# A two-layer trunk: where the weights of the next layer are split and where its residual is made

## The chip, the cores and the metric

The kernel runs on one core of a Trainium2 chip. The metric is the time of one execution on the device in microseconds, smaller is better; the figure given is the median of several runs. TensorE is the matmul engine (PE in the rows), VectorE is DVE, ScalarE is ACT, GpSimd is POOL, and SyncE (SP) only issues transfers here.

## What is computed

The reference, cut to the latent stream. All arrays are float32.

```python
alpha = (2 * DEPTH) ** 0.25                         # DEPTH = 2
h_lat = x                                           # [1, 512, 1024]
for layer in range(DEPTH):
    m_lat = split(silu(c) @ w_mod[layer] + b_mod[layer], 6)
    u_lat = h_lat * (1 + m_lat[1]) + m_lat[0]
    if layer == 0:                                  # attention beside a pooling mixer
        y_lat = attn_pool_mixer(u_lat, u_ctx, ...) @ w_out
    else:                                           # short gated convolution
        b_gate, c_gate, x_in = split(u_lat @ w_conv_in, 3)
        z = conv3(c_gate * x_in)                    # depthwise, width 3
        y_lat = (b_gate * z) @ w_conv_out
    h_lat = layer_norm(alpha * h_lat + m_lat[2] * y_lat, ln_mix_g, ln_mix_b)
    f_lat = expert_choice_ffn(h_lat * (1 + m_lat[4]) + m_lat[3], ...)   # 16 experts, 64 tokens each
    h_lat = layer_norm(alpha * h_lat + m_lat[5] * f_lat, ln_ffn_g, ln_ffn_b)
return h_lat
```

The convolution layer takes the normalised output of layer 0 twice: through the modulation into its input product, and, times alpha, as the residual that is added to the output projection.

## The kernel before

The 512 tokens are four row tiles of 128 (index `t`), the 1024 channels eight blocks of 128 (index `k`). Large weights stream from HBM into blocks of 16 KB per partition. `self.queue` lists what is loaded, in order; `next_load(b)` takes the next entry and loads it into block `b` as soon as the last reader of `b` is done, or, where the entry is `None`, puts `b` on the list `freed`. All these loads go through SyncE's queue. The order of instructions on each engine is the program's order (the schedule is written by hand); engines wait for one another only through data and buffers.

A float32 product of full precision outside the experts is made of three fast matmuls (`mm3`): both operands are split into a high part (a cast on ScalarE) and a low part (a subtract on VectorE or GpSimd). `split` does this (L247 the cast, L248 the subtract), and the three matmuls are L252 to L254.

**End of layer 0.** `moe(0)` runs 16 experts. In the last one, while the hidden copy `hT` waits for the down product, `ln_row` (L283, L285) spreads the LN gain and bias over all partitions: four matmuls into one PSUM bank and one ScalarE copy, twice for each of the two rows. They land in a spare block. Then the down product is made in two column halves (L1431), its sums are added to `A` (L1454, on VectorE; L1442 on GpSimd for two tiles), and the final norm follows in two halves of two row tiles each. Each tile has a reciprocal root (two ScalarE activations, then a Newton step on VectorE, L268 to L273) and a norm, L1563: `H = (A - mean) * rstd`, without the gain and bias.

`open_conv`, called before those norms, makes the first of the convolution's split weights: `prep_conv(i)` splits weight block `i` ([128 x 1024], three blocks per entry `ci0`, `ci1`, ... of the queue) into a ring of four slots. Blocks 0, 1 and 2 are split there, their subtracts on GpSimd; block 3 comes after the first two norms, also on GpSimd. `post1(b, g)` then turns half `b` of the tokens around: four transposes on TensorE, two scaled activations on ScalarE (L1607) and a split (`u1`, the low part on VectorE), for four groups `g`. `self.residual(t, g1)` computes `A = H * gain + bias` (both times alpha) with four GpSimd operations per row tile (L293, L294), tiles 0 and 1 after the first `post1`s, 2 and 3 at the very end.

**Layer 1.** `layer1_mixer` loops over `f` (8) and `b` (3): `conv_in` makes the product for weight block `i = 3f + b`, then `prep_conv(i + 3)` refills the ring, one step of the modulation's list `steps` runs (sums of gate weights on VectorE, L355 and L357; every third step a matmul `mod_b` or `mod_pc`), and VectorE works the convolution's taps (L1681 to L1687). For `f = 0` the products of the first 256 tokens run ahead of the rest. `mix_out` is the output projection: `project(t, n0, n1)` is one row tile times one column half, `evac` adds the result to the residual (L1092, L1096) and takes statistics; eight passes in all. At its start `others()` splits eight more weight tiles.

Of the kernel before, what the change touches and what calls it, by code (L numbers as in the profile page):

```python
# [16 lines left out]
P = 128  # L17
# [173 lines left out]
class Trunk:  # L191
    def __init__(self, nc, tc, ins, out, ctx):
        self.nc, self.tc, self.ins, self.out, self.ctx = nc, tc, ins, out, ctx
        self.n = 0
        self.last_tile = {}

# [253 lines left out]
    def run(self):  # L450
# [29 lines left out]
        def experts(l):  # L480
            return [item(f"{n}{l}_{e}_{h}", ins["wdl"][l, h] if (e, n) == (NE - 1, "d") else ins["w" + n][l, e, h])
                    for e in range(NE) for n in ("g", "u", "d") for h in range(2)]
# [6 lines left out]
        self.queue = ([m[0][i] for i in TN['order']] + [None] * 2 + m[1][:4] + experts(0) + ci[:4] + [None] * 4  # L489
                      + m[1][4:6] + [ci[4]] + m[1][6:8] + [ci[5], m[1][8], ci[6]] + m[1][9:11] + [ci[7], m[1][11]] + wco  # L490
# [546 lines left out]
    def mix_out(self, layer, aH, aL, w, others, sp, wk, mods, free):  # L1037
# [122 lines left out]

        for t in range(TT):
            p_y = project(t, 0, 512)
            if t == 0:
                consts()
                p_ls = [self.bank(q, (P, P), "p_l") for q in "gu"]
                p_f = [None] * TT
                p_a = self.bank("d", (64, 2 * P), "p_a")
            else:
                trans(t - 1, 0, 4)
            if t > 1:  # L1170
                logits(t - 2, 0)
            evac(t, 0, 512, p_y)
            if t == 0:
                others()
            step(t)
        for b in free[0]:
            self.next_load(b)
        for t in range(TT):
            lt = t == TT - 1
            for n0, n1 in ((512, 768), (768, 1024)) if lt else ((512, 1024),):  # L1180
# [12 lines left out]
                evac(t, n0, n1, p_y)  # L1193
                if n0 == 512 and lt:
                    softmax(0)()
# [80 lines left out]
    def moe(self, layer):  # L1276
# [6 lines left out]
        with tc.tile_pool(name=f"ex{layer}", bufs=2) as wk:  # L1283
# [87 lines left out]
            for e in range(NE):  # L1371
# [33 lines left out]
                if self.spare and not gb:  # L1405
                    gb += [self.spare[:, v * D:v * D + D] for v in range(2)]
                    g1 = [side(v) for v in gb]
                    for v in range(2):
                        self.ln_row(4 * layer + 2 + v, g1[v], 1.0 if last else ALPHA)
# [149 lines left out]
            else:  # L1559
# [12 lines left out]
                self.rs.append(self.prep_conv(3, nc.gpsimd))  # L1572
# [8 lines left out]
                for t in range(2):  # L1581
                    self.residual(t, g1)
# [6 lines left out]
                self.conv_in(self.p_c[1], self.rs[1], 0, 256)  # L1589
                for g in range(4):  # L1590
                    self.post1(1, g, wk)
                for t in range(2, TT):
                    self.residual(t, g1)
# [23 lines left out]
    def open_conv(self):  # L1617
# [3 lines left out]
        self.rs = [self.prep_conv(i, self.nc.gpsimd) for i in range(3)]  # L1621
        self.next_load(self.w["ci0"][1])
# [9 lines left out]
    def layer1_mixer(self):  # L1632
        nc, tc, ins, base = self.nc, self.tc, self.ins, self.base
        uH, uL = self.u1
        with tc.tile_pool(name="l1", bufs=1) as pool:
# [4 lines left out]
            hx = base.tile([P, TT, D], F32, tag="H", name="H")  # L1640
            self.H = hx
# [19 lines left out]
            for f in range(KO):  # L1661
# [4 lines left out]
                for b in range(3):  # L1666
                    i = 3 * f + b
                    p_b = self.bank(name=f"p_c{b}") if f else p_c[b]
                    self.conv_in(p_b, rs[i], 0 if f else 256, 512)
                    if i and i + 3 < 3 * KO:  # L1670
# [57 lines left out]
```

## Time and profile before

| what | value |
| --- | --- |
| median of 3 runs | 1466.15 us (1464.01 to 1473.38) |
| the profiled execution's own time | 1466.89 us |
| its span (first to last instruction) | 1465.0 us |
| TensorE busy | 1371.5 us |
| VectorE busy | 709.1 us |
| ScalarE busy | 335.2 us |
| GpSimd busy | 270.9 us |
| mean granted TensorE clock | 0.97 |

The table by stretches gives for each engine the busy us in a stretch and in brackets how many instructions, then the granted TensorE clock as a share of full speed. In the timeline each line has its start, its duration (or the extent of several merged instructions, with their count), engine, line of the kernel, operation, result and operands, and, in square brackets, how long the engine was idle before it and what ended that.

### The profile page before, as it was taken

To read this page: it belongs to the slowest core of one execution; us is meant where nothing else is said; L and a number is where in the kernel's file an instruction comes from. 1 tells how busy PE (TensorE), PEld (TensorE's weight loads), DVE (VectorE), ACT (ScalarE), POOL (GpSimd) and SP (SyncE) were. 2 spreads that over 40 slices of the span, in tenths; PEclk is the share of its full clock that TensorE was granted. 3 is DMA by queue.
4 is the path that set the end of the run, shared out by engine and by line. 5 is a ranking of instruction groups with operands and counts; after the bars stand their busy time and mean duration, and the time that the engine had idled before them with its cause. 6 is when DMAs were issued, how large, how long until landed. Compare 5 with 4: busy or idle time off the path is not lost.

```text
span 1465.0 us, 17481 instructions
## 1 busy us (share of the span) xinstructions
PE 1371.5 (94%) x7180; PEld 765.1 (52%) x7180; DVE 709.1 (48%) x1158; ACT 335.2 (23%) x661; POOL 270.9 (18%) x242
## 2 busy tenths in 40 slices
PE   7989998899999999999959999999999999999993
PEld 4866547654444444543348787764454454444332
DVE  3684768813343333342476799661243243343246
ACT  3455661311111011111043222231111111111013
POOL 2321628450000000000065445005000000000003
PEclk9989999999999999999979999999999999999996
DMA  9437337889999999999962554749999999999991
GB/s 370 159 133 284 140 138 318 310 325 407 428 425 427 427 427 427 426 426 427 417 271 98 230 211 172 287 191 376 427 427 426 426 428 426 427 426 427 426 388 57
DMA packets 42527, 490.35 MB, mean 335 GB/s; under 512 B 4752, under 2 KB 5200, under 8 KB 13136
## 3 DMA queue, kind: packets, MB, share of 16 engines
q1 hardware_dynamic: 41856, 486.10, 80.6%
q10 hardware_dynamic: 592, 3.15, 0.6%
q8 instruction: 56, 0.92, 0.3%
q14 instruction: 23, 0.19, 0.0%
HBM read 487.13 MB, written 2.10 MB: 334 GB/s over the span
## 4 chain that ended last, share of the span: by engine, by line
PE 66%; DMA 16%; DVE 13%; ACT 2%; issue 2%; SPq 0%; DVEq 0%; ACTq 0%
PE p_g L1331 11%; PE p_d L1331 11%; PE p_u L1331 10%; DMA blk<-wu 5%; DMA blk<-wg 5%; DMA blk<-wd 5%; PE p_ga_g L1309 5%; PE p_sc_sc L1359 3%; PE p_c_sc L252 2%; PE p_c_sc L253 2%; PE p_c_sc L254 2%; PE p_y_sc L252 2%; PE p_y_sc L254 2%; PE p_y_sc L253 2%; PE p_o L945 1%
## 5 line engine op out<-in xcount | busy, mean ns | idle before, releaser
L1331 PE MATMUL p_u<-blk,xe 128*64 128x512 f32 x1024 | 226.3, 593 | 6.3 <-DMA blk<-wu 6.3
L1331 PE MATMUL p_g<-blk,xe 128*64 128x512 f32 x1024 | 226.3, 593 | 2.2 <-ACT xe L1318 2.2
L1331 PE MATMUL p_d<-blk,hT 128*64 128x512 f32 x960 | 215.2, 601 | 0.0
L1391 DVE TENSOR_TENSOR rows<-sg,p_u 128x512 f32<-128x512 f32 x32 | 22.0, 688 | 325.4 <-PE p_u L1331 315.3
L1362 DVE SCALAR_TENSOR_TENSOR A<-p_sc_sc,gates,A 128x512 f32<-128x512 f32 x240 | 163.2, 743 | 6.1 <-PE p_sc_sc L1359 6.1
L1331 PEld LDWEIGHTS p_u<-blk,xe 128*64 128x64 f32 x1024 | 72.4, 137 | 154.5 <-issue 140.0
L1331 PEld LDWEIGHTS p_g<-blk,xe 128*64 128x64 f32 x1024 | 72.6, 137 | 147.1 <-issue 140.0
L1421 POOL COPY m5c<-m5b 64x256 f32<-64x256 f32 x8 | 3.2, 394 | 718.0 <-PE p_ga_g L1309 717.6
L1331 PEld LDWEIGHTS p_d<-blk,hT 128*64 128x64 f32 x960 | 66.6, 138 | 131.4 <-issue 131.2
L1318 ACT ACTIVATE xe<-p_ga_g,FG 128x128 f32<-128x128 f32 x112 | 42.2, 457 | 306.8 <-PE p_ga_g L1309 306.8
L1309 PEld LDWEIGHTS p_ga_g<-sel,H 128*128 128x128 f32 x896 | 104.2, 192 | 3.0 <-issue 0.8
L1309 PE MATMUL p_ga_g<-sel,H 128*128 128x128 f32 x896 | 104.7, 275 | 0.0
L1353 ACT CAST yp<-rows 64x512 fp32r<-64x512 f32 (+1 forms) x68 | 40.2, 591 | 272.8 <-DVE rows L1350 272.0
L1350 DVE TENSOR_TENSOR rows<-p_d,m5b 128x512 f32<-128x512 f32 x30 | 20.8, 692 | 136.3 <-PE p_d L1331 136.3
L1359 PE MATMUL p_sc_sc<-yp,st 128*128 128x512 f32 x240 | 72.8, 421 | 1.0 <-DVE A L1362 1.0
L248 POOL TENSOR_TENSOR blk<-blk,blk 128x1024 fp32r<-128x1024 f32 (+1 forms) x25 | 59.7, 2405 | 67.8 <-ACT blk L247 67.8
L252 PE MATMUL p_c_sc<-blk,blk 128*128 128x512 f32 x168 | 67.7, 403 | 0.0
L253 PE MATMUL p_c_sc<-blk,blk 128*128 128x512 f32 x168 | 65.9, 392 | 0.0
L254 PE MATMUL p_c_sc<-blk,blk 128*128 128x512 f32 x168 | 65.8, 392 | 0.0
L1359 PEld LDWEIGHTS p_sc_sc<-yp,st 128*128 128x128 f32 x240 | 40.6, 188 | 34.3 <-issue 24.3
L1354 DVE TENSOR_TENSOR yp<-rows,yp 64x512 fp32r<-64x512 f32 (+1 forms) x68 | 45.6, 671 | 25.3 <-ACT yp L1353 24.2
L357 DVE SCALAR_TENSOR_TENSOR rows<-blk,cond,rows 128x512 f32<-128x512 f32 x49 | 56.2, 1147 | 1.5
(402 smaller groups left out, 1999.3 us busy)
## 6 DMA issues: line engine op xcount, KB each, us to landing
blk<-wg SPq DMA_DIRECT2D x60, 2048.0 KB, 28.0
blk<-wu SPq DMA_DIRECT2D x60, 2048.0 KB, 22.1
blk<-wd SPq DMA_DIRECT2D x56, 2048.0 KB, 26.3
blk<-wmod SPq DMA_DIRECT2D x23, 2048.0 KB, 8.7
blk<-wci SPq DMA_DIRECT2D x8, 1536.0 KB, 12.2
blk<-wd SPq DMA_DIRECT2D x8, 1024.0 KB, 7.2
blk<-wg SPq DMA_DIRECT2D x8, 1024.0 KB, 8.7
blk<-wu SPq DMA_DIRECT2D x16, 512.0 KB, 22.9
```

Of the source, the lines that this page charges most:

```text
L248: (eng or nc.vector).tensor_tensor(lo, src, hi.bitcast(F32), ALU.subtract)
L252: mm(out, ah, bh, start=start, stop=False)
L253: mm(out, ah, bl, start=False, stop=False)
L254: mm(out, al, bh, start=False, stop=stop)
L357: nc.vector.scalar_tensor_tensor(a, W[:, k], c, a, ALU.mult, ALU.add)
L1309: nc.tensor.matmul(pg[:, j - j0], H[:, t, j * P:(j + 1) * P], sels[g][:, t, e0:e1].rearrange("p e s -> p (e s)"), start=t == 0, stop=t == ...
L1318: nc.scalar.activation(o, pg[:, j - j0], AF.Identity, bias=self.FG[:, 1, j:j + 1], scale=self.FG[:, 0, j:j + 1])
L1331: nc.tensor.matmul(o[64 * hf:64 * hf + 64], lhs(k), W[:, kk, hf * 512:hf * 512 + 512], start=k == 0, stop=k == KO - 1)
L1353: nc.scalar.copy(yp[r, hf], ye[r])
L1354: nc.vector.tensor_tensor(yp[q, hf], ye[r], yp[r, hf].bitcast(F32), ALU.subtract)
L1359: nc.tensor.matmul(pp[hf], st[:, t * P:(t + 1) * P], yp[:, hf], start=True, stop=True)
L1362: nc.vector.scalar_tensor_tensor(a, pp[hf], self.gateT[:, t, e:e + 1], a, ALU.mult, ALU.add)
```

## The change

Four things change. In the queue the fourth convolution weight (`ci3`) and the first gate weight of layer 1 (`m[1][4]`) trade places. At the end of layer 0 only weight block 0 is split beside the norms; GpSimd takes block 1 after a one-element copy that reads the second norm's result, VectorE takes block 2 after the second pair of norms, and GpSimd block 3 between the second and third group of the second half. The load that reuses `ci0`'s block follows block 2. The residual leaves GpSimd: the old `H` is kept under the name `A`, the new scratch tile takes the buffer of the old `A`, and VectorE multiplies and adds in place, in eight pieces of one row tile and one column half, two before the first pass of `mix_out` and one after each evacuation. The LN rows for it are made in the convolution's steps 1 and 2 instead of in the last expert of layer 0.

```diff
--- before.py
+++ after.py
@@ -193,6 +193,7 @@
         self.nc, self.tc, self.ins, self.out, self.ctx = nc, tc, ins, out, ctx
         self.n = 0
         self.last_tile = {}
+        self.resid = []
 
 
     def cv(self, name, rows=P):
@@ -486,8 +487,8 @@
         wco = [item(f"wco{h}", ins["wco"][h]) for h in range(2)]
         self.item, self.mitems = item, m
         self.w, self.freed = {}, []
-        self.queue = ([m[0][i] for i in TN['order']] + [None] * 2 + m[1][:4] + experts(0) + ci[:4] + [None] * 4
-                      + m[1][4:6] + [ci[4]] + m[1][6:8] + [ci[5], m[1][8], ci[6]] + m[1][9:11] + [ci[7], m[1][11]] + wco
+        self.queue = ([m[0][i] for i in TN['order']] + [None] * 2 + m[1][:4] + experts(0) + ci[:3] + m[1][4:5] + [None] * 4
+                      + [ci[3], m[1][5], ci[4]] + m[1][6:8] + [ci[5], m[1][8], ci[6]] + m[1][9:11] + [ci[7], m[1][11]] + wco
                       + experts(1))
         self.layer0_mixer()
         self.moe(0)
@@ -1158,6 +1159,11 @@
             for i, s in plan[q] if mods else ():
                 mods[i][s]()
 
+        def resid(n=1):
+            for _ in range(min(n, len(self.resid))):
+                self.resid.pop(0)()
+
+        resid(2)
         for t in range(TT):
             p_y = project(t, 0, 512)
             if t == 0:
@@ -1170,6 +1176,7 @@
             if t > 1:
                 logits(t - 2, 0)
             evac(t, 0, 512, p_y)
+            resid()
             if t == 0:
                 others()
             step(t)
@@ -1191,6 +1198,7 @@
                 else:
                     softmax(1)()
                 evac(t, n0, n1, p_y)
+                resid()
                 if n0 == 512 and lt:
                     softmax(0)()
             if lt:
@@ -1402,11 +1410,11 @@
                 if e < NE - 1:
                     scatters(2)
                 st = scatter_sel(e)
-                if self.spare and not gb:
+                if last and self.spare and not gb:
                     gb += [self.spare[:, v * D:v * D + D] for v in range(2)]
                     g1 = [side(v) for v in gb]
                     for v in range(2):
-                        self.ln_row(4 * layer + 2 + v, g1[v], 1.0 if last else ALPHA)
+                        self.ln_row(4 * layer + 2 + v, g1[v], 1.0)
                 lhs = lambda k: hT[:, k % 4, (k // 4) * CAP:(k // 4) * CAP + CAP]
                 yp = wk.tile([P, 2, 512], F32R, name="yp", bufs=1)
                 if e < NE - 1:
@@ -1569,7 +1577,9 @@
                 for t in range(2):
                     newton[t]()
                     norm(t)
-                self.rs.append(self.prep_conv(3, nc.gpsimd))
+
+                nc.gpsimd.tensor_copy(self.smc[:, 3:4], H[:, 1, D - 1:D])
+                self.rs.append(self.prep_conv(1, nc.gpsimd))
                 for t in (2, 3):
                     nc.vector.bn_stats(bst[:, t, 0], A[:, t, 0:512])
                 total(2)
@@ -1578,8 +1588,6 @@
                 total(3)
                 for g in range(2, 4):
                     self.post1(0, g, wk)
-                for t in range(2):
-                    self.residual(t, g1)
                 rstd(2, 4)()
                 for t in (2, 3):
                     norm(t)
@@ -1587,10 +1595,12 @@
                 self.p_c = [self.bank(q, name="p_c") for q in "gud"]
                 self.conv_in(self.p_c[0], self.rs[0], 0, 256)
                 self.conv_in(self.p_c[1], self.rs[1], 0, 256)
+                self.rs.append(self.prep_conv(2))
+                self.next_load(self.w["ci0"][1])
                 for g in range(4):
                     self.post1(1, g, wk)
-                for t in range(2, TT):
-                    self.residual(t, g1)
+                    if g == 1:
+                        self.rs.append(self.prep_conv(3, nc.gpsimd))
 
     def post1(self, b, g, wk):
 
@@ -1618,8 +1628,7 @@
 
         self.rblk, self.ublk = self.freed[-4:-2], self.freed[-2:]
         self.ring = [self.block(b, F32R).rearrange("p (i s k c) -> p i s k c", i=2, s=2, k=KO) for b in self.rblk]
-        self.rs = [self.prep_conv(i, self.nc.gpsimd) for i in range(3)]
-        self.next_load(self.w["ci0"][1])
+        self.rs = [self.prep_conv(0, self.nc.gpsimd)]
         self.u1 = [self.block(b, F32R).rearrange("p (k n) -> p k n", k=KO) for b in self.ublk]
 
     def prep_conv(self, i, eng=None):
@@ -1637,8 +1646,17 @@
             gL = pool.tile([P, KO, S], F32R, name="gL")
             rx, ry = self.rblk
 
-            hx = base.tile([P, TT, D], F32, tag="H", name="H")
-            self.H = hx
+            hx = base.tile([P, TT, D], F32, tag="A", name="A")
+            self.H, self.A = hx, self.H
+            gb = [[pool.tile([P, 512], F32, name=f"l1gb{v}{h}") for h in range(2)] for v in range(2)]
+
+            def residual(h, t):
+                a = self.A[:, t, h * 512:h * 512 + 512]
+                nc.vector.tensor_tensor(a, a, gb[0][h], ALU.mult)
+                nc.vector.tensor_tensor(a, a, gb[1][h], ALU.add)
+
+            self.resid = [lambda q=q: residual(*divmod(q, TT)) for q in range(2 * TT)]
+
             self.load_gates(1, hx[:, 3])
             cbs, zbs = ([hx[:, a, i * 512:i * 512 + 512] for i in range(2)] for a in range(2))
             tb = hx[:, 2, 0:S + 2]
@@ -1667,6 +1685,8 @@
                     i = 3 * f + b
                     p_b = self.bank(name=f"p_c{b}") if f else p_c[b]
                     self.conv_in(p_b, rs[i], 0 if f else 256, 512)
+                    if i in (1, 2):
+                        self.ln_row(1 + i, gb[i - 1], ALPHA)
                     if i and i + 3 < 3 * KO:
                         rs.append(self.prep_conv(i + 3, nc.gpsimd if i > 1 else None))
                     elif i + 3 >= 3 * KO:
```

## Rows read from the trace of the kernel before

**Rows 1.** The page's list of engines: busy us (share of the span) and instructions.

```profile
PE 1371.5 (94%) x7180; PEld 765.1 (52%) x7180; DVE 709.1 (48%) x1158; ACT 335.2 (23%) x661; POOL 270.9 (18%) x242
```

**Rows 2.** Stretches: busy us of PE, PEld, DVE, ACT, POOL; PE clock; DMA share; GB/s.

```profile
746.00:755.50 9.50, 0.01 (x1) 0.00 (x0) 9.19 (x15) 3.33 (x7) 9.01 (x4) 0.53 0.72 266
...
765.80:767.80 2.00, 0.00 (x0) 0.00 (x0) 1.93 (x6) 0.79 (x3) 1.34 (x2) 0.81 0.00 0
767.80:774.70 6.90, 6.87 (x35) 6.88 (x36) 2.68 (x7) 0.00 (x0) 4.57 (x4) 0.56 0.01 2
...
818.50:902.00 83.50, 83.50 (x386) 69.54 (x385) 72.46 (x75) 17.49 (x21) 42.13 (x20) 1.00 0.56 221
...
921.00:972.00 51.00, 50.38 (x309) 41.10 (x309) 28.43 (x79) 12.53 (x32) 0.72 (x3) 1.00 0.52 193
...
957.00:961.00 4.00, 4.00 (x20) 3.30 (x19) 1.24 (x8) 1.65 (x3) 0.00 (x0) 1.00 0.00 0
```

**Rows 3.** Waits of TensorE, 740 to 830: total us, times, longest.

```profile
PE p_tr_sc L1603 <- DVE H L1563: 12.4, 2, 9.6
PE p_c_g L253 <- DVE blk L248: 3.5, 4, 2.1
PE mod_b_sc L415 <- DVE rows L357: 2.1, 1, 2.1
```

**Rows 4.** The timeline of VectorE (start, us, ...): norms and Newton steps of both halves.

```profile
749.35 1.09 DVE L268 SCALAR_TENSOR_TENSOR rs_t<-l_r 128x1 f32<-128x1 f32 x1
...
750.66 2.08 DVE L273 TENSOR_TENSOR l_r<-l_r,rs_t 128x1 f32<-128x1 f32 x1
752.77 2.79 DVE L1563 TENSOR_SCALAR H<-A,l_nm,l_r 128x1024 f32<-128x1024 f32 x1
...
756.96 1.84 DVE L1563 TENSOR_SCALAR H<-A,l_nm,l_r 128x1024 f32<-128x1024 f32 x1
...
768.30 0.15 DVE L270 TENSOR_TENSOR rs_t<-l_r 128x2 f32<-128x2 f32 x1
...
768.88 0.16 DVE L273 TENSOR_TENSOR l_r<-l_r,rs_t 128x2 f32<-128x2 f32 x1
769.08 1.54 DVE L1563 TENSOR_SCALAR H<-A,l_nm,l_r 128x1024 f32<-128x1024 f32 x2
```

**Rows 5.** The timeline of GpSimd: weight splits, and the residual's last operation.

```profile
745.77 9.24 POOL L248 TENSOR_TENSOR blk<-blk,blk 128x1024 fp32r<-128x1024 f32 x4 [1.40 <-ACT blk L247]
...
780.10 1.62 POOL L294 TENSOR_TENSOR A<-A,blk 128x512 f32<-128x512 f32 x1
```

**Rows 6.** The chain that ended last, in order of time: the LN rows.

```profile
732.83 1.73 PE p_gb_sc L283 x16
```

**Rows 7.** The timeline of SyncE's queue: the last expert's down weights.

```profile
719.67 9.24 SPq L215 DMA_DIRECT2D blk<-wdl  x8
```

**Rows 8.** Transfers issued 719.6 to 729: count, KB each, us to landing.

```profile
blk<-wdl SPq DMA_DIRECT2D x8, 512.0 KB, 10.2
```

**Rows 9.** The timeline of VectorE: low halves of activations, and a later one.

```profile
761.95 2.78 DVE L248 TENSOR_TENSOR blk<-u1t,blk 128x512 fp32r<-128x512 f32 x2
...
766.54 1.84 DVE L248 TENSOR_TENSOR blk<-u1t,blk 128x512 fp32r<-128x512 f32 x2
...
777.12 5.75 DVE L248 TENSOR_TENSOR blk<-u1t,blk 128x512 fp32r<-128x512 f32 x4 [6.50 <-ACT blk L247]
...
798.83 0.69 DVE L248 TENSOR_TENSOR gL<-H,gH 128x512 fp32r<-128x512 f32 x1 [0.81 <-ACT gH L247]
```

**Rows 10.** The timeline of ScalarE: the LN rows' copies; the cast of block 4.

```profile
733.26 2.07 ACT L285 ACTIVATE blk<-p_gb_sc 128x512 f32<-128x512 f32 x4 [10.53 <-DMA blk<-wdl]
...
784.41 1.05 ACT L247 CAST blk<-blk 128x1024 fp32r<-128x1024 f32 x1
```

**Rows 11.** The timeline of VectorE: an addition in the convolution, one evacuation.

```profile
801.46 0.69 DVE L417 TENSOR_TENSOR H<-mod_b_sc,H 128x512 f32<-128x512 f32 x1 [1.94 <-PE mod_b_sc L415]
...
942.03 0.69 DVE L1092 TENSOR_TENSOR blk<-p_y_sc,H 128x512 f32<-128x512 f32 x1 [4.26 <-PE p_y_sc L254]
```

## Prediction

> **What bounds the kernel now.** I read the page first: TensorE is busy for most of the span [rows 1], so a change pays only where TensorE stands idle or runs at the lower of its two clock levels. The table by stretches shows where that is. From 818.5 to 902 TensorE has no gap at the full clock; from 746 to 755.5 it does nothing, from 765.8 to 767.8 it stands again, and behind that, to 774.7, it works at a mean granted clock of 0.56, so mostly at 1.2 of its 2.4 GHz [rows 2]. So the seam between the layers is the stretch to look at. TensorE's waits there name the cause: 12.4 us for the norm's result `H`, 3.5 us for the low halves of the split activations, and 2.1 us further on for a VectorE sum [rows 3].
>
> The timeline of VectorE shows why `H` is late. From 749.35 to 758.80 it does only two Newton steps and two norms. The same lines run again later, where GpSimd is idle: the [128x1024] norm takes 2.79 and 1.84, but two later ones 1.54 together; a one-column multiply takes 2.08, against 0.16 for the later one of two columns [rows 4]. GpSimd runs four weight splits of 2.31 us each from 745.77 to 755.01, and behind them the residual's sixteen multiplies and adds, the last ending at 781.72 [rows 5]. So VectorE stands behind GpSimd, instruction by instruction.
>
> **The change part by part.** I time all from the second norm's end (758.80 before) or from named starts.
>
> *a. No LN rows in the last expert of layer 0.* Sixteen matmuls, 1.73 us on the chain, stand between the hidden copy and the down product [rows 6]. They go; the product starts 1.73 earlier. It mustn't overtake its weights: the eighth `wdl` transfer is issued at about 728.6 and takes 10.2, so it is there near 738.8 [rows 7, 8]; the last quarter of the product follows the first sums, past 739.4 even with the gain. Gain 1.7; the bound below is 0, if that transfer is later than its median.
>
> *b. One split instead of four beside the norms.* GpSimd keeps `prep_conv(0)` (745.77 to 748.08, or 1.7 earlier), which is over when the first Newton step starts. The one-column copy into `smc` holds the next split until the second norm has been written. The later Newton step has four operations from 768.30 to the norm's start at 769.08, 0.78; these have three, so about 0.6. A free norm is 0.77. Twice that is 2.75, against 758.80 - 749.35 = 9.45 [rows 4]. Gain 6.7. The bound above is this; the bound below is 4.4, if one more split of 2.3 still hits the chain.
>
> *c. The first half's splits and its 48 matmuls.* Four low-half splits took 2.78 + 1.84 = 4.62 beside the residual; a free one is 0.69, four are 2.76 [rows 9]. That is 1.9 saved at most; ScalarE, which makes the groups one after another, may keep some 0.4 of it (an estimate). So the low half for which TensorE waited until 767.8, 9.0 after the second norm, comes about 7.5 after it. Gain 1.5, bounds 0 and 1.9. Behind that wait 35 matmuls took 6.9 us at a mean clock of 0.56 [rows 2]: 6.9 x 0.56 = 3.9 at the full clock, 7.7 at half. The wait before them shrinks a little from its 2.0, so the clock may fall in it again or not. I take a gain of 0.5, nearer to what the row shows, with bounds -0.8 and +3.0.
>
> The second half's norms end some 3 us before TensorE asks for them, and `prep_conv(2)`, moved to VectorE behind them, is one [128x1024] subtract, about 1.4 (two free [128x512] ones), done before its use. Both cost nothing; the cover is the 24 matmuls of the second weight block, and without it the 1.4 would be paid.
>
> *d. `prep_conv(3)` between the groups of the second half.* Its cast on ScalarE takes 1.05, as that of the next block does [rows 10], ahead of the third group's activations, and its split on GpSimd 2.3 beside VectorE's third low half. Before, these four low halves took 5.75 beside the residual, now gone [rows 9]; three free ones and one behind the split come to about 4.5, but they wait for ScalarE, whose last group is 1.05 later. The bound below is therefore 0 (the 5.75 - 4.5 pays for it), the bound above 2.4, a whole split more. I take the cast: cost 1.1. The Trainium skill (SBUF — State Buffer, Who interferes with whom) says that a VectorE operation with two SBUF inputs blocks until a GpSimd instruction that reads SBUF and began first is over as a whole. By that rule d could cost all of the 2.4 and the sum below would be 6.0 instead of 7.3; the trace agrees in so far as one column took 2.08 beside splits of 2.31 [rows 4, 5], but the row of four shows 1.4 each on the mean.
>
> *e. The LN rows inside the convolution.* Two times eight matmuls, 1.73 in all, now stand behind the second and third products, where TensorE has no gap. Worse is ScalarE's queue: the two copies of a row (2.07 for four) are issued ahead of the cast for `prep_conv(4)`. That cast ran at 784.41, right behind the first product [rows 10]; now it stands behind the second product (24 matmuls, 2.9 at the 0.12 us to which 3.9 / 35 comes) and the copies (1.0). VectorE's chain (split, sums of the gate weights, convolution taps) is in program order behind it and starts 3.8 later. It leads to the `mod_b` matmul at 814.4 for which TensorE already waits 2.1 [rows 3]. On the way VectorE idles 1.94 before L417 [rows 11], which takes up half. Cost 1.8, bounds 0 (the row's matmuls then fill TensorE's old wait) and 3.8.
>
> *f. The residual on VectorE.* Sixteen operations of about 0.69 = 11.0 us. From 921 to 972 VectorE is busy 28.4 of 51 us and waits for TensorE before most evacuations (4.26 in the row shown) [rows 2, 11]. Only in the first two passes, which hold eight more splits, do they queue: the second evacuation comes some 3 us late, and the transposes behind the third pass may wait 0.2. Cost 0.2; the bound above is 11.0, were none of it hidden. The sixteen GpSimd operations removed cost nothing where they stood, beyond b to d; the new `H` tile is free earlier, which nobody waits for.
>
> *g. Queues.* One `wmod` block (2 MB) now follows three `wci` blocks, where a fourth `wci` (1.5 MB) stood; the displaced `wci` block comes when `prep_conv(2)` has read the first. The first use of the `wmod` block is some 20 us after its landing, that of the late `wci` block in the third convolution step. SP's later transfers keep their order. What this saves must still reach the end: layer 1's experts stream their weights, and that stream must start earlier too. It can, as the transfers stand still before it (share 0.00 from 957 to 961 [rows 2]) until the output projection frees blocks. Cost 0; without that the whole gain would be lost in the experts' loads.
>
> Sum: 1.7 + 6.7 + 1.5 + 0.5 - 1.1 - 1.8 - 0.2 = 7.3 us. The profiled execution took 1466.89 (span 1465.0), so 1459.6; the median of the runs shown lies 0.7 below it, so I forecast 1459.0.
>
> **The rivals.** *1. The convolution gives it back.* The delay of e is not absorbed, and d is at its bound: costs 2.4 + 3.8 + 0.2 against 10.4 leave 4.0, and 2.3 with the weights of a late: 1462 to 1464. For it: TensorE already waits for VectorE there [rows 3]; against: VectorE's idle 1.94 [rows 11].
>
> *2. The clock holds through the first half.* The 35 matmuls of c save 3.0 instead of 0.5 and d hides in part: gain 10 to 12, so 1454 to 1456. For it: a shorter idle stretch; against: the clock was low behind a gap of 2.0, about the same size [rows 2]. The Trainium skill (TensorE: Matmul & The Clock Gate, What's actually happening) says that the points at which the clock can change don't follow the kernel's start; no row of one execution can show it, and the number above doesn't rest on it.
>
> *3. Slower: the residual lands on the path.* If the project passes wait for it pass by pass, up to 11.0 is paid against 7.5, so up to 1469.6. It decides once over 7.5 of the 11.0 are unhidden. Against: 22.6 idle us of VectorE in that stretch, and TensorE is idle there for only 0.6 [rows 2].
>
> *4. VectorE isn't freed.* If the slow norms were not GpSimd's doing, b and c go and the rest is 1.7 - 3.1, a loss of 1.4: 1467.6. Against: the same line at 0.77 and 2.79.
>
> **How the numbers follow.** The forecast (1456.5 to 1461.5) gets 0.55, rival 1 0.20, rival 2 0.13, rival 3 0.05, rival 4 0.07. The range holds the first three: the bounds in favour of a to c give 1.7 + 6.7 + 1.9 + 3.0 = 13.3 at no cost, so 1453; a at 0 with d and e at their bounds leaves 2.3, so 1464. I give 1453.0 to 1464.0; rivals 3 and 4 are left out. One per cent is 14.7 us, about what a measurement of this kernel can tell from no change; even all bounds together don't reach it. So within 1% gets 0.92, faster 0.04, slower 0.04.
>
> **What would show it.** Right: the norms at 0.8 us and the second one ending near 750.5; TensorE's wait for `H` at about 6 us less; its transposes of the second half near 764 and the wait at `mod_b` (L415) at 2 us or more. Wrong: norms still near 2 us (b); a wait for `wdl` in the down product (a); the second transposes later than 766 (c); VectorE's sums ending over 4 us later after the first product (e); project passes that wait for VectorE (f).

## The result and the profile after

The changed kernel takes 1458.03 us (median of 8 runs, 1454.91 to 1459.45) against 1467.13 for the kernel before (8 runs); the ratio is 0.9933, with a 95% interval of 0.9916 to 0.9949. That is 9.1 us by the medians, or 0.7%, and the interval lies clear of 1. The forecast was 1459.0, a gain of 7.3 us. The ratios of the experiments below are likewise to the kernel before, measured beside each variant on the same chip; one kernel's median differs by up to 1.7 us from one set of runs to the next (1458.03 and 1456.30 for the changed kernel), so a small difference of times across sets says little.

The profiled execution took 1459.45 (span 1457.7). The lines of VectorE that answer to [rows 4] and [rows 9] come first; line numbers are those of the changed kernel, so L269 is the old L268, L274 the old L273, L1571 the old norm L1563, and L249 the old subtract L248.

```profile
749.37 0.21 DVE L269 SCALAR_TENSOR_TENSOR rs_t<-l_r 128x1 f32<-128x1 f32 x1
...
749.80 0.16 DVE L274 TENSOR_TENSOR l_r<-l_r,rs_t 128x1 f32<-128x1 f32 x1
750.00 0.81 DVE L1571 TENSOR_SCALAR H<-A,l_nm,l_r 128x1024 f32<-128x1024 f32 x1
...
751.35 0.81 DVE L1571 TENSOR_SCALAR H<-A,l_nm,l_r 128x1024 f32<-128x1024 f32 x1
...
755.32 0.69 DVE L249 TENSOR_TENSOR blk<-u1t,blk 128x512 fp32r<-128x512 f32 x1
...
758.93 1.35 DVE L249 TENSOR_TENSOR blk<-u1t,blk 128x512 fp32r<-128x512 f32 x2
```

A Newton step and a norm are at their free durations now, both of them, and the second norm is over at 752.16, 2.79 us after the first Newton step began (9.45 before). The low halves of the first half's activations are 0.69 each. GpSimd's timeline in the same stretch, which answers to [rows 5], shows why:

```profile
745.78 2.35 POOL L249 TENSOR_TENSOR blk<-blk,blk 128x1024 fp32r<-128x1024 f32 x1 [1.40 <-ACT blk L248]
752.23 0.18 POOL L1581 COPY smc<-H 128x1 f32<-128x1 f32 x1 [4.10 <-DVE H L1571]
752.37 2.36 POOL L249 TENSOR_TENSOR blk<-blk,blk 128x1024 fp32r<-128x1024 f32 x1
```

One split ahead of the norms, the one-element copy that waits for the second norm, one split behind it, and no residual. The stretches (columns as in [rows 2]) show TensorE:

```profile
745.00:750.80 5.80, 1.03 (x6) 0.66 (x5) 5.01 (x16) 2.39 (x6) 2.35 (x1) 0.66 1.02 429
...
758.10:759.60 1.50, 0.31 (x2) 0.11 (x1) 1.43 (x6) 1.47 (x4) 0.00 (x0) 1.00 0.00 0
759.60:764.00 4.40, 4.34 (x36) 4.34 (x37) 3.91 (x9) 1.20 (x3) 0.00 (x0) 1.00 0.02 4
...
773.60:806.60 33.00, 30.21 (x162) 25.56 (x161) 25.34 (x29) 8.58 (x12) 10.18 (x4) 1.00 0.33 126
...
896.50:910.20 13.70, 13.66 (x50) 10.05 (x51) 11.53 (x18) 4.42 (x8) 2.05 (x4) 0.88 0.45 154
```

In the second of these rows TensorE has finished a last matmul at 758.41 and then stands 1.25 us for the third low half, until 759.66; before, that wait was 2.06 (765.77 to 767.83). The clock stays at full behind it, and the 35 matmuls that took 6.9 us [rows 2] take 4.3 (759.66 to 763.96). But the stretch from the first product to step 6's `mod_b` matmul now holds a longer wait than in [rows 3], 2.9 instead of 2.1; the waits of TensorE from 730 to 815:

```profile
PE p_tr_sc L1613 <- DVE H L1571: 5.7, 2, 4.8
PE mod_b_sc L416 <- DVE rows L358: 2.9, 1, 2.9
PE p_c_g L254 <- DVE blk L249: 2.3, 2, 1.2
```

To compare executions I use six marks: the start of the selection matmul of the last expert (`p_sb`), the first Newton step, the second norm's end, the second half's transposes, ScalarE's copy of the first product, and the `mod_b` matmul of step 6. The stretches between them, worked out from starts in the timelines, repeat within 0.1 us from execution to execution of one kernel unless the clock differs, while the execution's own time scatters by some microseconds elsewhere:

| kernel | p_sb to Newton | to second norm's end | to second transposes | to first product's copy | to mod_b, step 6 | sum |
| --- | --- | --- | --- | --- | --- | --- |
| before | 16.90 | 9.45 | 15.98 | 9.15 | 30.47 | 81.95 |
| before, a second execution | 16.89 | 9.47 | 14.82 | 9.94 | 30.49 | 81.61 |
| after | 15.16 | 2.79 | 11.80 | 9.66 | 33.05 | 72.46 |
| after, a second execution | 15.15 | 2.80 | 11.80 | 9.64 | 33.08 | 72.47 |
| four_splits | 15.16 | 7.87 | 11.79 | 8.71 | 33.06 | 76.59 |
| seam_traffic | 15.15 | 2.80 | 14.56 | 10.22 | 33.12 | 75.85 |
| no_gate | 15.16 | 4.76 | 11.80 | 9.65 | 33.05 | 74.42 |
| rows_back | 16.90 | 2.79 | 11.80 | 9.65 | 33.05 | 74.19 |
| no_resid | 15.16 | 2.79 | 11.80 | 9.65 | 33.05 | 72.45 |
| rows_in_waits | 15.16 | 2.80 | 11.79 | 9.65 | 31.06 | 70.46 |
| block3_early | 15.16 | 2.80 | 11.79 | 8.71 | 33.05 | 71.51 |
| both | 15.17 | 2.80 | 11.80 | 8.70 | 31.05 | 69.52 |
| rows_after_cast | 15.15 | 2.80 | 11.79 | 9.65 | 30.03 | 69.42 |
| rows_and_block3 | 15.16 | 2.80 | 11.80 | 8.70 | 30.04 | 68.50 |

So the five stretches are worth 81.95 - 72.46 = 9.49 us, near the 9.1 of the medians. The two profiled spans differ by 7.3 only, mostly because the whole of layer 0 up to the first mark, where nothing was changed, ran 1.76 us later in this execution (734.21 against 732.45).

### The profile page after: what moved, and what is told of

It reads as the page before. It is cut to its first block, busy times and chain, and to the rows that moved or that the text cites. A ratio compares the mean times of both kernels' runs of the same rounds, so it can differ in the third digit from the quotient of the medians.

```text
span 1457.7 us, 17479 instructions
## 1 busy us (share of the span) xinstructions
PE 1368.7 (94%) x7180; PEld 763.2 (52%) x7180; DVE 709.2 (49%) x1175; ACT 335.3 (23%) x661; POOL 246.5 (17%) x226
## 4 chain that ended last, share of the span: by engine, by line
PE 66%; DMA 17%; DVE 12%; ACT 2%; issue 2%; POOL 0%; SPq 0%; DVEq 0%; ACTq 0%; POOLq 0%
PE p_g L1339 11%; PE p_d L1339 11%; PE p_u L1339 10%; DMA blk<-wu 5%; DMA blk<-wg 5%; DMA blk<-wd 5%; PE p_ga_g L1317 5%; PE p_sc_sc L1367 3%; PE p_y_sc L253 2%; PE p_c_sc L253 2%; PE p_c_sc L254 2%; PE p_c_sc L255 2%; PE p_y_sc L255 2%; PE p_y_sc L254 2%; PE p_o L946 1%
## 5 line engine op out<-in xcount | busy, mean ns | idle before, releaser
L1370 DVE SCALAR_TENSOR_TENSOR A<-p_sc_sc,gates,A 128x512 f32<-128x512 f32 x120 | 81.6, 742 | 3.0 <-PE p_sc_sc L1367 3.0
L1370 DVE SCALAR_TENSOR_TENSOR H<-p_sc_sc,gates,H 128x512 f32<-128x512 f32 x120 | 81.6, 742 | 3.0 <-PE p_sc_sc L1367 3.0
L249 POOL TENSOR_TENSOR blk<-blk,blk 128x1024 fp32r<-128x1024 f32 (+1 forms) x24 | 58.1, 2435 | 83.6 <-ACT blk L248 83.6
L1389 ACT ACTIVATE sg<-p_g 128x512 f32<-128x512 f32 x32 | 19.1, 597 | 154.3 <-PE p_g L1339 154.3
L1317 PEld LDWEIGHTS p_ga_g<-sel,A 128*128 128x128 f32 x448 | 52.1, 192 | 1.9 <-issue 0.8
## 6 DMA issues: line engine op xcount, KB each, us to landing
blk<-wu SPq DMA_DIRECT2D x16, 512.0 KB, 22.8
```

Of the source, the lines that this page charges most:

```text
L249: (eng or nc.vector).tensor_tensor(lo, src, hi.bitcast(F32), ALU.subtract)
L1317: nc.tensor.matmul(pg[:, j - j0], H[:, t, j * P:(j + 1) * P], sels[g][:, t, e0:e1].rearrange("p e s -> p (e s)"), start=t == 0, stop=t == ...
L1370: nc.vector.scalar_tensor_tensor(a, pp[hf], self.gateT[:, t, e:e + 1], a, ALU.mult, ALU.add)
```

## The experiments

**Which GpSimd work holds VectorE up.** The theory was that GpSimd's instructions do; the rival, that the gain comes from the moved rows or the moved residual. The first run puts the splits back and leaves the residual where the change has it.

```diff
-        self.rs = [self.prep_conv(0, self.nc.gpsimd)]
+        self.rs = [self.prep_conv(i, self.nc.gpsimd) for i in range(3)]
-                nc.gpsimd.tensor_copy(self.smc[:, 3:4], H[:, 1, D - 1:D])
-                self.rs.append(self.prep_conv(1, nc.gpsimd))
+                self.rs.append(self.prep_conv(3, nc.gpsimd))
-                self.rs.append(self.prep_conv(2))
-                    if g == 1:
-                        self.rs.append(self.prep_conv(3, nc.gpsimd))
```

> The changed kernel, but with all four weight splits on GpSimd where the kernel before has them (blocks 0 to 2 ahead of the norms, block 3 behind the first two). The residual stays on VectorE in the output projection. Theory (GpSimd's splits hold VectorE up): from the first Newton step's start to the second norm's end 9.4 us again instead of 2.8; from that start to the second half's transposes some 21 instead of 14.6, or 23 if the clock falls; time 6 to 9 us above the changed kernel, so 0 to 3 below the kernel before. Rival (the gain comes from the residual's or the LN rows' move): 2.8 and 14.6 as they are, time within 2 us of the changed kernel.

It measured 1462.45 us, ratio 0.9959 (0.9944 to 0.9975), and 7.87 us for the norms. VectorE's timeline:

```profile
752.11 2.07 DVE L274 TENSOR_TENSOR l_r<-l_r,rs_t 128x1 f32<-128x1 f32 x1
754.22 2.79 DVE L1571 TENSOR_SCALAR H<-A,l_nm,l_r 128x1024 f32<-128x1024 f32 x1
...
757.56 0.81 DVE L1571 TENSOR_SCALAR H<-A,l_nm,l_r 128x1024 f32<-128x1024 f32 x1
```

The first Newton step and norm are slow as before, the second norm is free. So the splits cost 7.87 - 2.79 = 5.08 of term b, and the remaining 1.6 (9.45 - 7.87) was the residual, which in the kernel before had begun on the first tile while the second was still being normed:

```profile
755.64 1.26 POOL L293 TENSOR_TENSOR A<-H,blk 128x512 f32<-128x512 f32 x1 [0.63 <-DVE H L1563]
756.98 1.26 POOL L294 TENSOR_TENSOR A<-A,blk 128x512 f32<-128x512 f32 x1
...
755.92 1.00 DVE L273 TENSOR_TENSOR l_r<-l_r,rs_t 128x1 f32<-128x1 f32 x1
```

The first of them runs beside the second Newton multiply (the VectorE line, 1.00 instead of 0.16), the second beside the second norm (1.84 from 756.96, [rows 4]). The expected 9.4 was too much by this, and so was the expected loss of 6 to 9 us: the five stretches are 4.1 longer than in the changed kernel. The theory itself stands, the rival's 2.8 did not come. TensorE's part behind the norms, 11.79, is that of the changed kernel.

The second run gives the seam the residual's traffic back and leaves the splits alone:

```diff
+                for t in range(2):
+                    for h in range(2):
+                        s = slice(h * 512, h * 512 + 512)
+                        nc.gpsimd.tensor_tensor(A[:, t, s], H[:, t, s], H[:, t, s], ALU.mult)
+                        nc.gpsimd.tensor_tensor(A[:, t, s], A[:, t, s], H[:, t, s], ALU.add)
```

> The changed kernel plus eight GpSimd operations of [128x512] behind the first half's four groups, in the form and place of the old residual of row tiles 0 and 1; what they write is not used. Theory (the residual cost the seam its splits and the clock): the norms stay at 0.8 us, the four low halves of the first half go from 0.7 each to 1.0 to 1.4, the second half's transposes come 1.5 us later at full clock and up to 4 later if the clock falls. Rival (the residual was harmless there, only the weight splits were not): transposes within 0.3 us, time the same as the changed kernel's.

It measured 1459.18 us, ratio 0.9946 (0.9920 to 0.9972), which settles nothing by itself; the marks do. The second transposes come 14.56 - 11.80 = 2.8 later, and the first product behind them loses 0.6 more. VectorE's low halves, and the stretches around TensorE's wait:

```profile
755.69 1.53 DVE L249 TENSOR_TENSOR blk<-u1t,blk 128x512 fp32r<-128x512 f32 x1 [0.16 <-ACT blk L248]
...
759.03 2.44 DVE L249 TENSOR_TENSOR blk<-u1t,blk 128x512 fp32r<-128x512 f32 x2
```

```profile
758.20:760.00 1.80, 0.06 (x1) 0.00 (x0) 1.73 (x6) 1.43 (x4) 1.79 (x2) 0.92 0.00 0
760.00:763.00 3.00, 2.93 (x13) 2.84 (x14) 2.97 (x4) 0.52 (x1) 2.92 (x3) 0.50 0.03 5
```

Low halves of 1.53 and 1.2 (two in 2.44) lengthen TensorE's wait from 1.25 to 1.81 us (758.26 to 760.07); the mean clock of 0.92 in that stretch says that it fell near its end, and it is at half from 760 to 763. Of the 2.8, 1.15 lie ahead of the third low half's matmul and 1.6 behind it, where the clock is low. This is one execution; but the eleven in the table with free low halves kept the clock here, so the residual's move is what keeps it.

The third run takes the gate away, a single line:

```diff
-                nc.gpsimd.tensor_copy(self.smc[:, 3:4], H[:, 1, D - 1:D])
```

> The changed kernel without the one-element copy that holds GpSimd's second weight split until the second norm is written. Its cast ends at about 750.9, so the split then runs beside the second Newton step and the second norm. Theory: the second norm ends about 2 us later (one GpSimd instruction of 2.35 is waited for once), and everything to the end of the seam shifts by 1.5 to 2. Rival (the copy does nothing, as ScalarE's cast paces that split): the second norm within 0.3 us, time the same.

It measured 1461.74 us, ratio 0.9951 (0.9936 to 0.9967). The norms' end is 1.97 later:

```profile
752.27 2.13 DVE L274 TENSOR_TENSOR l_r<-l_r,rs_t 128x1 f32<-128x1 f32 x1
754.44 0.81 DVE L1571 TENSOR_SCALAR H<-A,l_nm,l_r 128x1024 f32<-128x1024 f32 x1
```

One multiply of a single column waits 2 us, for one split of 2.34 (752.05 to 754.39), and the norm behind it is free again. The two share no data and no buffer, so engines here wait for one another by a third way besides the two that the description of the kernel names. The Trainium skill (SBUF — State Buffer, Who interferes with whom) says that a VectorE operation with two SBUF inputs contends with a GpSimd instruction that reads SBUF, and that the later one waits until the earlier is over; this row agrees. It also says that an operation with at most one SBUF input, outside the two-port modes, does not contend: the statistics of the changed kernel (two in 1.28 from 752.08) ran beside a GpSimd split at their usual speed. The norm, with one [128x1024] input and two single columns, does wait (2.79 in the first run above, 0.81 when free); by which side of the rule, no row shows.

**The LN rows of layer 0.**

```diff
-                if last and self.spare and not gb:
+                if self.spare and not gb:
```

> The changed kernel, in which the last expert of layer 0 makes the LN rows as well, into the spare block as before; they are not used. Theory (term a is worth its 1.7 us): from the hidden copy's end to the first Newton step 16.9 us instead of 15.2, time 1.7 above the changed kernel. Rival (the down product waits for its weights anyway): 15.2 to 15.6, time the same.

It measured 1460.94 us, ratio 0.9945 (0.9930 to 0.9961); the first stretch is 16.90 instead of 15.16, so term a is 1.74. The rows are on the chain again, with the same 1.73 as in [rows 6]:

```profile
734.69 1.73 PE p_gb_sc L284 x16
```

**What the moved rows cost in the convolution.** My reason was ScalarE's queue. In the changed kernel it reads (it answers to [rows 10]):

```profile
767.75 1.04 ACT L248 CAST blk<-blk 128x1024 fp32r<-128x1024 f32 x1
...
773.62 0.59 ACT L1699 COPY A<-p_c_g 128x512 f32<-128x512 f32 x1 [1.68 <-PE p_c_g L255]
776.89 1.09 ACT L286 ACTIVATE l1gb<-p_gb_sc 128x512 f32<-128x512 f32 x2 [2.69 <-PE p_gb_sc L284]
777.86 1.05 ACT L248 CAST blk<-blk 128x1024 fp32r<-128x1024 f32 x1
```

The cast of weight block 4 (777.86) runs 4.24 us after the copy of the first product instead of 0.48, behind the rows' copies. The fifth run puts the rows where TensorE waits anyway:

```diff
-                    if i in (1, 2):
-                        self.ln_row(1 + i, gb[i - 1], ALPHA)
...
+                    if i in (6, 21):
+                        self.ln_row(2 + (i > 6), gb[i > 6], ALPHA)
                     for _ in range((0, 1, 1, 0, 1, 2)[i] if i < 6 else 1):
```

> The changed kernel with the two LN rows made in the convolution's steps 6 and 21, right ahead of the matmuls (mod_b) for which TensorE waits there, instead of in steps 1 and 2. Theory (ScalarE's queue: the rows' copies hold up the cast of weight block 4 and with it VectorE's chain): from the end of the first convolution product to the mod_b matmul of step 6 31 us instead of 33, and the rows fit into the two waits; time 1.5 to 2.5 below the changed kernel. Rival (the rows cost only TensorE's 1.7 us, wherever they stand): the first stretch 1.0 to 1.7 shorter, but both given back at the two waits, time the same.

It measured 1460.00 us, ratio 0.9952 (0.9934 to 0.9970), so it isn't faster. The stretch to `mod_b` is 2.0 shorter, as the theory said, but the next one, to the `mod_pc` matmul of step 9, takes 21.06 instead of 18.40. TensorE's timeline and the clock behind it:

```profile
803.44 1.46 PE L416 MATMUL mod_b_sc<-rows,cst 128*128 128x512 f32 x2 [1.81 <-DVE A L1707]
805.53 0.79 PE L253 MATMUL p_c_sc<-blk,blk 128*128 128x512 f32 x1 [0.63 <-ACT l1gb L286]
```

```profile
806.00:808.00 2.00, 2.00 (x6) 1.52 (x6) 0.00 (x0) 1.39 (x2) 1.98 (x2) 0.50 1.01 426
```

The first row's eight matmuls do fit into the wait. But they take PSUM banks from the pool of four that `mod_b` uses: by its releaser, the `mod_b` matmul now waits for the bank that L1707 frees, which VectorE runs only behind the sums, and the next product waits 0.63 for the rows' copies. Behind that the clock is at half. This fall isn't the moved rows' alone. The same stretch, from `mod_b` of step 6 to `mod_pc` of step 9, in the changed kernel, in its second execution, in the run with block 3 early (below; its rows stand in steps 1 and 2) and in this run:

```profile
806.67:825.07 18.40, 17.47 (x75) 13.82 (x75) 11.33 (x16) 4.05 (x5) 7.15 (x3) 1.00 0.58 229
...
805.49:824.43 18.94, 18.94 (x75) 15.19 (x76) 12.44 (x16) 4.05 (x5) 7.14 (x3) 0.91 0.57 222
...
806.18:826.41 20.23, 20.23 (x75) 15.80 (x75) 12.99 (x17) 5.62 (x7) 7.26 (x4) 0.85 0.61 227
...
803.44:824.50 21.06, 20.43 (x75) 15.74 (x76) 12.66 (x16) 6.58 (x9) 7.30 (x4) 0.84 0.58 217
```

With the rows in steps 1 and 2 ahead of the split, the clock fell behind the 2.9 us wait of step 6 in six of eight executions, in one of them for as long as here. So of the 2.66 us lost here, about 0.8 (21.06 - 20.23) is the moved rows' own; whether they also make the longer fall likelier is not shown. The rival's result came out, by a way it hadn't named. The later test of the same reason leaves the rows in steps 1 and 2 and only issues them behind the split, so that ScalarE's cast goes first:

```diff
-                    if i in (1, 2):
-                        self.ln_row(1 + i, gb[i - 1], ALPHA)
                     if i and i + 3 < 3 * KO:
                         rs.append(self.prep_conv(i + 3, nc.gpsimd if i > 1 else None))
...
+                    if i in (1, 2):
+                        self.ln_row(1 + i, gb[i - 1], ALPHA)
                     for _ in range((0, 1, 1, 0, 1, 2)[i] if i < 6 else 1):
```

> The changed kernel with the LN rows in the same steps 1 and 2, but issued behind the weight split of the step, so that ScalarE makes the cast of block 4 first and the rows' copies after it. TensorE's order is the same. Theory (term e is the queue of ScalarE, not TensorE's sixteen matmuls): from the end of the first product to the mod_b matmul of step 6 some 30.5 us again, as in the kernel before, instead of 33.0; TensorE's wait there 0.3 instead of 2.9, and the clock holds; time 2.5 below the changed kernel. Rival (the rows cost TensorE's 1.7 us in any order): 32 to 33, time the same.

It measured 1454.09 us, ratio 0.9912 (0.9890 to 0.9934); the changed kernel measured again on the same chip gave 1456.30, ratio 0.9927 (0.9903 to 0.9950). ScalarE, and VectorE behind it:

```profile
778.65 0.59 ACT L1699 COPY A<-p_c_g 128x512 f32<-128x512 f32 x1 [1.68 <-PE p_c_g L255]
779.13 1.05 ACT L248 CAST blk<-blk 128x1024 fp32r<-128x1024 f32 x1
781.92 1.09 ACT L286 ACTIVATE l1gb<-p_gb_sc 128x512 f32<-128x512 f32 x2 [1.74 <-PE p_gb_sc L284]
```

```profile
797.96 0.69 DVE L418 TENSOR_TENSOR A<-mod_b_sc,A 128x512 f32<-128x512 f32 x1 [4.59 <-PE mod_b_sc L416]
```

The cast comes 0.48 after the copy again, VectorE waits 4.59 for TensorE instead of TensorE for VectorE, and the stretch is 30.03. The intervals of the two ratios overlap, so it is the stretch, 3.0 shorter, that shows the gain and not the time. TensorE's sixteen matmuls are still there and in the same order: term e was the queue, as the theory said.

**Weight block 3.**

```diff
                 self.rs.append(self.prep_conv(2))
+                self.rs.append(self.prep_conv(3))
...
-                    if g == 1:
-                        self.rs.append(self.prep_conv(3, nc.gpsimd))
```

> The changed kernel with weight block 3 split by ScalarE and VectorE right behind block 2, while both engines are idle ahead of the second half's transposes, instead of by ScalarE and GpSimd between the groups of the second half. Theory (term d is ScalarE's cast of 1.05 between the groups): from the second transposes' start to the first product's end 9.0 instead of 9.7 us, time 0.7 below the changed kernel. Rival (the stretch is bound elsewhere, or VectorE's longer queue delays block 2's product): 9.7 or more, time the same or up to 1 above.

It measured 1458.58 us, ratio 0.9948 (0.9927 to 0.9969), no visible gain in time; in the profiled execution the fall of the clock behind step 6 (20.23 instead of 18.40, above) costs more than the edit gains. The stretch from the second transposes to the first product is 8.71 instead of 9.66, 0.3 less than expected. VectorE splits blocks 2 and 3 in its idle time, and the third low half isn't held up:

```profile
762.88 2.35 DVE L249 TENSOR_TENSOR blk<-blk,blk 128x1024 fp32r<-128x1024 f32 x2
...
769.91 0.69 DVE L249 TENSOR_TENSOR blk<-u1t,blk 128x512 fp32r<-128x512 f32 x1 [0.88 <-ACT blk L248]
```

The 0.95 is the cast and the one contended low half (1.40 in the changed kernel).

**The residual in the output projection.**

```diff
             def residual(h, t):
                 a = self.A[:, t, h * 512:h * 512 + 512]
-                nc.vector.tensor_tensor(a, a, gb[0][h], ALU.mult)
-                nc.vector.tensor_tensor(a, a, gb[1][h], ALU.add)
+                pass
```

> The changed kernel without the sixteen VectorE operations of the residual in the output projection (gain and bias of the first layer's last norm are left out of it). Theory (term f: they lie beside the matmuls): from the first to the second transposes of the output projection 5.9 us as it is, time within 0.5 us of the changed kernel. Rival (they are on the path): time 3 to 11 us below the changed kernel.

It measured 1458.34 us, ratio 0.9944 (0.9925 to 0.9962). From the second `mod_b` matmul of the last gate block to the first comparison of the routing it is 59.27 us, against 59.29 with the residual and 59.26 in the kernel before; the first and second transposes lie 5.93 apart with it and without it. TensorE's waits in that part are those of the changed kernel:

```profile
PE p_a_d L1152 <- DVE o_r L1115: 0.7, 1, 0.7
PE p_tr_sc L1121 <- DVE H L1097: 0.6, 1, 0.6
```

**Versions that may beat both.** The first joins the rows in steps 6 and 21 with block 3 on VectorE:

> The changed kernel with both moves together: LN rows in steps 6 and 21, weight block 3 on VectorE ahead of the second half. Theory: the two gains add, 2.2 to 3.2 us below the changed kernel, so about 1455. Rival: they go into the same wait at the mod_b matmul, time 1.5 below it or less.

It measured 1456.97 us, ratio 0.9929 (0.9904 to 0.9954): the five stretches are 2.94 shorter, but in the profiled execution the stretch from `mod_b` to `mod_pc` behind step 6 takes 21.29 instead of 18.40, which is nearly all of it. The second joins the two edits that held:

> The kernel of the run before this one, and weight block 3 split on VectorE ahead of the second half. Theory: both gains add, 2.5 + 0.9 = 3.4 us below the changed kernel, about 1455. Rival (a later wait takes them): less than 1.5 below it.

It measured 1452.60 us, ratio 0.9902 (0.9881 to 0.9922), 3.7 below the changed kernel on the same chip; the five stretches are 3.97 shorter. It has the lowest median of all, though its interval overlaps that of the kernel with only the rows issued later. TensorE's waits, 735 to 925:

```profile
PE p_tr_sc L1612 <- DVE H L1571: 5.6, 2, 4.8
...
PE p_c_g L254 <- DVE blk L249: 1.6, 2, 1.2
PE mod_pc_sc L322 <- DVE rows L358: 0.9, 1, 0.9
```

The wait at step 6 is gone.

**Was the fall of the clock in the kernel before a chance?**

> The kernel before, unchanged, profiled a second time. Theory (the long wait for the third low half makes the clock fall there each time, as it did in the run with the residual's traffic): the clock falls in the 2 us wait again, and from the first Newton step to the second half's transposes it is 25.4 us again, within 0.3. Rival (the fall was one execution's chance): the clock holds, and that stretch is some 2.6 shorter.

> The changed kernel, unchanged, on the chip of the two runs that follow. Theory: 14.6 us from the first Newton step to the second half's transposes at the full clock, 2.6 us more than before from the end of the first product to the mod_b matmul; 8 to 10 us below the kernel before. Rival (the clock held by chance): the stretch is 17 us in this execution.

For the kernel before, theory and rival both missed. Its second execution took 1469.75 us (a single run), and 24.29 from the first Newton step to the second transposes, between the 25.4 of the theory and the 22.8 of the rival:

```profile
767.00:768.00 1.00, 0.00 (x0) 0.00 (x0) 0.96 (x4) 0.41 (x2) 0.99 (x1) 1.00 0.00 0
...
769.00:770.00 1.00, 1.00 (x9) 1.00 (x9) 0.86 (x6) 0.00 (x0) 0.00 (x0) 0.85 0.07 16
...
771.00:772.00 1.00, 1.00 (x7) 1.00 (x7) 0.38 (x1) 0.00 (x0) 1.00 (x1) 0.50 0.00 0
```

TensorE's wait of 2 us is there (767 to 768), the clock falls behind it, but some 2 us later than in the first execution, so that only part of the 35 matmuls ran at half. The changed kernel had 14.6 in both executions, and 11.8 behind the norms in every variant with free low halves, eleven executions in all.

## Why the prediction was right

**a.** 1.7 predicted, 1.74 measured by the first stretch and by putting the rows back. The weights were there in time; no wait for `wdl` appeared.

**b.** 6.7 predicted, 6.66 measured. The sum from free durations was right; what I didn't see is that 1.6 of it belongs to the residual and not to the splits.

**c.** This is the term that was mis-sized. The low half came 7.5 after the second norm (752.16 to 759.66), as worked out. But I took 0.5 for the clock, "nearer to what the row shows", and measured 2.6 against the first execution (6.9 to 4.3), near the upper bound that made rival 2. The step that failed is the judgement that the wait shrinks "a little" and leaves the clock's fall open: it shrank from 2.06 to 1.25, with free low halves the clock held in all eleven executions, and with the residual's traffic back it fell. Against the second execution of the kernel before the same term is worth 1.5, so the size isn't a constant. The bound itself was a little off: 6.9 x 0.56 = 3.9 takes a matmul at half clock for twice as long, but the starts are 0.213 apart at half (768.63 to 773.54 before) and 0.12 at full (760.00 to 763.84 after), so the 35 take 4.3 at full.

**d.** 1.1 predicted, 0.51 measured (9.15 to 9.66). The cast's cost was right (0.95 when it is moved away), but I left the residual's share at its bound of nothing; it gave back 0.44. Against the second execution of the kernel before (9.94) d is even a gain of 0.3, as c is smaller there.

**e.** 1.8 predicted, 2.58 measured. The delay of VectorE's chain was 3.8, as worked out; what it found idle ahead of the `mod_b` addition (L417 before, L418 now) was less than I took:

```profile
792.93 0.69 DVE L418 TENSOR_TENSOR A<-mod_b_sc,A 128x512 f32<-128x512 f32 x1 [0.82 <-PE mod_b_sc L416]
```

It idles 0.82 there instead of 1.94 [rows 11], so only 1.1 was absorbed and not 2.0.

**f.** 0.2 predicted, nothing measurable (0.02). A piece of the residual on VectorE's line in the output projection, and the evacuations of the fourth pass, which [rows 11] showed, and of the fifth:

```profile
915.73 0.68 DVE L1655 TENSOR_TENSOR H<-H,l1gb 128x512 f32<-128x512 f32 x1
...
935.09 0.69 DVE L1093 TENSOR_TENSOR blk<-p_y_sc,A 128x512 f32<-128x512 f32 x1 [1.24 <-PE p_y_sc L255]
...
941.54 0.69 DVE L1093 TENSOR_TENSOR blk<-p_y_sc,A 128x512 f32<-128x512 f32 x1 [2.94 <-PE p_y_sc L255]
```

The wait of 4.26, at the fourth pass, shrank to 1.24, and that at the fifth from 4.25 to 2.94, which is where the residual went.

**g.** As predicted; neither of the two loads that traded places is waited for. VectorE does wait for a later `wmod` load, 6.06 us at 815.26, but so it did before (5.57), and TensorE's wait behind it, at `mod_pc`, is 0.92 here and 0.94 in the second execution of the kernel before. The gain also reached the end: from the top-k to the last instruction it is 488.2 us, 488.6 before.

The sum to step 6 was 7.5 predicted and 9.49 measured: c was 2.2 too small, d 0.6 too large, e 0.8 too small. Behind step 6, up to the last gate block's second `mod_b`, the executions of these two kernels differ by up to 2.4 us (102.7 to 105.2) with the clock, which falls or doesn't fall at the remaining waits of 2 to 3 us; in the profiled execution of the changed kernel it fell near 897 (0.88 in the table above), in its second one behind step 6 instead (0.91 in the rows of that stretch). My sum has no term for this.

The time came nearer than the sum: 1.0 from the forecast, where the sum was 1.8 short of the medians' 9.1. Part of that is luck. The forecast started from 1466.3, and the kernel before measured 1467.13 beside the change, 0.8 more; and e's error took back part of those of c and d. The sign "second half near 764" (763.96) also came out only because layer 0 ran 1.76 us later in this execution; without that it is 762.2.

## What to carry to other kernels

Where VectorE is on the path and GpSimd works beside it, price the path from free durations and count the GpSimd instructions that can start in it; a copy that reads the last result of the path holds a whole GpSimd queue back for almost nothing. Work moved into the shadow of a matmul stream must be placed with regard to each queue it passes: sixteen matmuls cost nothing there, and the two copies ahead of one cast cost 2.6 us until they were issued behind it. When a wait shrinks, look what the clock did behind the old one: the matmuls that follow can be worth more than the wait.

## What the runs showed that I hadn't expected

TensorE's clock held across idle stretches of 1.25 us in eleven executions, and fell in or behind stretches of 1.8 to 2.1 us in all three executions that had one at this place, with partly filled stretches ahead of them. In the convolution it differs from execution to execution: behind step 6's wait of 2.1 in the kernel before it was at half in the first (0.50 from 814.9 to 818.2) and full in the second, and behind the wait of 2.9 in the changed kernel full in the first and at half in the second. A short wait filled with matmuls can still end later than an empty one, when these take the PSUM bank that the next matmul needs, as in step 6 of rows_in_waits.
